# Variance along rows on one core: another split of columns between DVE, ACT and GpSimd, and the first loads' section under SP

## The chip, the cores and the metric

One core of a Trainium2 chip runs the program. The metric is the device time of one execution in microseconds. The kernel before takes 163.88 us, the median of 3 runs (163.84 to 163.9).

In the profile's names, ACT is ScalarE, DVE is VectorE, POOL is GpSimd, and SP is SyncE, which here issues the DMAs; "DVEq", "ACTq" and "SPq" are the instruction sequencers of the engines. TensorE is not used.

## The reference

```python
def setup_inputs():
    batch, seq, dim = 32, 512, 1024
    return {"x": np.random.randn(batch, seq, dim).astype(np.float32)}

def reference(x):
    mean_sq = np.mean(x**2, axis=-1)
    sq_mean = np.mean(x, axis=-1)**2
    return (mean_sq - sq_mean).astype(np.float32)
```

For each of 32 x 512 = 16384 rows of 1024 numbers the result is the mean of the squares less the square of the mean, that is, the variance of the row. The input is 67.1 MB, the output 65.5 KB.

## The kernel before

**Columns.** The 16384 rows are spread over 128 partitions and 128 columns: one column is one row of x on every partition, 128 x 1024 numbers in float32, 512 KB. All results stand in `mv[:, 1, c]`, one number per partition and column.

**Stages.** Columns 0 to 95 go through a loop in groups of 16 (`GROUP`), 8 MB a group, through two buffers `xt[0]` and `xt[1]` (`NBUF`). Three turns of the loop (`TURNS`) take two groups each. The 32 columns behind them (`END0` = 96 onwards) are the tail. It is loaded in eight loads of 8, 8, 5, 4, 2, 2, 1 and 1 columns (`END_LOADS`), and the very last column in two pieces of 512 numbers (`PIECES`). The first 16 tail columns go into `xt[0]`, the rest into `xt_end`.

**Two ways to a variance.** DVE takes a column with two `bn_stats` of 512 numbers each (the helper `halves`, line 118), and one `bn_aggr` that joins the two sets of statistics (line 225 in the loop, 253 and 267 in the tail). ACT takes a column with two passes: `act_mean` (line 122) sums the row into a scaled negative mean, `act_var` (line 127) squares the row with this mean as bias and sums again. Each pass is two instructions in the profile, an ACTIVATE and an ACTIVATION_READ_ACCUMULATOR that writes the sum. ACT works in batches: all means of a batch, a wait, all variances of it.

**Who takes what.** In the loop ACT has the first 6 of the 16 columns of a group (`NACT`), in two batches of 3 (`ACT_BATCH`), and DVE the other 10. In the tail, the string `END_WHO` gives each column of each load to A (ACT) or D (DVE). The first 11 D columns (`JOINED`, all those of the first two loads) get only their `bn_stats` on DVE; GpSimd joins their statistics in eleven small steps on all of them at once (lines 181 to 210), the last two of them writing one run of neighbouring columns each. For the other nine D columns DVE does the `bn_aggr` itself; it is put off behind the first `bn_stats` of the next column (`waiting`).

**Order.** All loads and stores are issued by SP, in program order, into one queue. The first two group loads stand in a `tile_critical` section (line 149), behind which the barriers of `tc.close()` and `tc.compile()` follow. Then SP loads a group as soon as the group two before it is finished: it waits on `done` (line 157). The first tail load waits for the fifth group (line 159); the other tail loads are issued right behind it.

In the loop DVE waits for the landing of a group, increments `go`, on which ACT starts its columns of that group, and does 20 `bn_stats` and 10 `bn_aggr`. Ahead of the last `bn_aggr` it waits for ACT's `act_done` (line 224); the last `bn_aggr` increments `done`. After every second group GpSimd copies the variances from `stage` to `mv` (line 174).

```python
            for j in mine:
                if j == mine[-1]:
                    take(dve, act_done, 1)
                last = dve.bn_aggr(out=stage[:, j, :], in_=stats[:, j, :, :])
            last.then_inc(done, 1)
```

DVE and ACT run through the tail in their own program order, each waiting for `landed_end[b]` ahead of its first column of load `b`. SP issues three stores: columns 0 to 15 (line 306), columns 16 to 120 when GpSimd's joined columns, ACT's of the first four loads and DVE's up to the fifth load are there (lines 307 to 310), and columns 121 to 127 when ACT and DVE are through (lines 311 to 313).

`addr_align` (line 147) places the code of ACT and DVE from that point on at instruction 128 of a fetch block.

Of the kernel before, what the change touches and what calls it, by code (L numbers as in the profile page):

```python
# [11 lines left out]
def kernel(  # L12
# [15 lines left out]
    P = nc.NUM_PARTITIONS  # L28
    FP32 = mybir.dt.float32
    ACTF = mybir.ActivationFunctionType  # L30
    ALU = mybir.AluOpType
    ENG = mybir.EngineType

    xf = x.flatten_outer_dims()
    N, D = xf.shape
    assert N % P == 0
    ncols = N // P
# [6 lines left out]
    GROUP = 16  # L44
    NBUF = 2
    TURNS = 3
    PER_TURN = NBUF * GROUP
    END0 = TURNS * PER_TURN
    NACT = 6
    ACT_BATCH = 3  # L50
    END_LOADS = [8, 8, 5, 4, 2, 2, 1, 1]
    END_WHO = "AADDDDDD" "AAADDDDD" "AADDD" "AADD" "DD" "AD" "D" "A"
    FIRST = END_LOADS[0] + END_LOADS[1]
    JOINED = END_WHO[:FIRST].count("D")
    PIECES = [512, 512]
    EARLY = 4
    HEAD = 128
# [1 line left out]
    def sbuf(name, shape, dtype):  # L59
        return nc.alloc_sbuf_tensor(name, shape, dtype).ap()  # L60

    def psum(name, shape, dtype):
        return nc.alloc_psum_tensor(name, shape, dtype).ap()

    xt = [sbuf(f"xt{b}", [P, GROUP, D], FP32) for b in range(NBUF)]
    xt_end = sbuf("xt_end", [P, ncols - END0 - FIRST, D], FP32)
    mv = sbuf("mv", [P, 2, ncols], FP32)
    stage = sbuf("stage", [P, PER_TURN, 2], FP32)
    stats = sbuf("stats", [P, PER_TURN, 2, 6], FP32)
    stats_join = sbuf("stats_join", [P, JOINED, 2, 6], FP32)  # L70
    stats_end = sbuf("stats_end", [P, ncols - END0, 4, 6], FP32)
    neg_mean = sbuf("neg_mean", [P, PER_TURN], FP32)
    neg_mean_end = sbuf("neg_mean_end", [P, ncols - END0], FP32)
    two = sbuf("two", [P, JOINED, 2], FP32)
    mu = sbuf("mu", [P, JOINED, 1], FP32)
    dev = sbuf("dev", [P, JOINED, 4], FP32)
    junk = [sbuf(f"junk{i}", [P, D], mybir.dt.bfloat16) for i in range(ACT_BATCH)]
    junk_sq = [psum(f"junk_sq{i}", [P, D], FP32) for i in range(ACT_BATCH)]

    sync, act, dve, gps = nc.sync, nc.scalar, nc.vector, nc.gpsimd  # L80
    landed = [nc.alloc_semaphore(f"landed{b}") for b in range(NBUF)]
    NEND = len(END_LOADS) + len(PIECES)
    landed_end = [nc.alloc_semaphore(f"landed_end{b}") for b in range(NEND)]
# [10 lines left out]
    def load(dst, c0, n, sem, f0=0, f=D):  # L94
        b0, pitch, row0 = next(b for b in BLOCKS if b[0] <= c0 < b[0] + b[1])
        assert c0 + n <= b0 + pitch
        ap = [[pitch * D, P], [D, n], [1, f]] if n > 1 else [[pitch * D, P], [1, f]]
        sync.dma_start(  # L98
            out=dst,
            in_=dataclasses.replace(xf, offset=(row0 + c0 - b0) * D + f0, ap=ap),  # L100
        ).then_inc(sem, 16)
# [10 lines left out]
    def take(engine, sem, n):  # L112
        engine.wait_ge(sem, n)
        engine.sem_inc(sem, -n)  # L114
# [6 lines left out]
    def act_mean(i, xcol, nm):  # L121
        return act.activation(  # L122
            out=junk[i], in_=xcol, func=ACTF.Copy, scale=-S / D, accum_out=nm
        )

    def act_var(i, xcol, nm, var):
        return act.activation(  # L127
            out=junk_sq[i], in_=xcol, func=ACTF.Square, scale=S, bias=nm, accum_out=var
        )

    def end_col(c):
        k = c - END0
        return xt[0][:, k, :] if k < FIRST else xt_end[:, k - FIRST, :]

    end_cols = []
    at = END0
    for b, n in enumerate(END_LOADS):
        end_cols += [(b, c, END_WHO[c - END0]) for c in range(at, at + n)]
        at += n
    assert at == ncols - 1 and sum(PIECES) == D  # L140
    early = END0 + sum(END_LOADS[:EARLY])
    act_step_of, dve_step_of = {}, {}
    joined = [c for b, c, who in end_cols if who == "D"][:JOINED]
    assert joined[-1] < END0 + FIRST and TURNS * NBUF >= NBUF + 1

    for engine in (act, dve):
        engine.addr_align(FETCH_BLOCK_INSTRUCTIONS, offset=HEAD, max_nops=0)

    with tc.tile_critical(sync_engine=ENG.Pool, no_gpsimd_drain=True):
        for g in range(NBUF):  # L150
            load(xt[g], g * GROUP, GROUP, landed[g])
    ctx.close()
# [7 lines left out]
    c = END0  # L160
    for b, n in enumerate(END_LOADS):
        k = c - END0
# [3 lines left out]
    f = 0  # L166
    for b, n in enumerate(PIECES, len(END_LOADS)):
        load(end_col(c)[:, f : f + n], c, 1, landed_end[b], f, n)
        f += n

    gps.sem_inc(copied, 1)
    for t in range(TURNS):
# [11 lines left out]
        lambda: gps.tensor_scalar(out=mu, in0=mu, scalar1=0.25, scalar2=None, op0=ALU.mult),  # L184
        lambda: gps.tensor_tensor(out=dev, in0=mean, in1=mu.to_broadcast([P, JOINED, 4]), op=ALU.subtract),
        lambda: gps.tensor_tensor(out=dev, in0=dev, in1=dev, op=ALU.mult),
# [25 lines left out]
    with nc.Fori(0, TURNS, engines=[ENG.DVE]):  # L212
        take(dve, copied, 1)
        for b in range(NBUF):
            take(dve, landed[b], 16)
            dve.sem_inc(go, 1)
            mine = range(b * GROUP + NACT, (b + 1) * GROUP)
            for j in mine:
# [11 lines left out]
    for b, c, who in end_cols:  # L230
        if who != "D":
            continue
        if b != seen:
            dve.wait_ge(landed_end[b], 16)
            seen = b
        col = end_col(c)
        if c in joined:
            last = halves(stats_join[:, joined.index(c), :, :], col)
            if c == joined[-1]:
                last.then_inc(dve_step, 1)  # L240
                n += 1
            continue
        st = stats_end[:, c - END0, :2, :]
        dve.bn_stats(out=st[:, 0, :], in_=col[:, :H])  # L244
        if waiting:
            waiting()
        n += 1
        dve.bn_stats(out=st[:, 1, :], in_=col[:, H:]).then_inc(dve_step, 1)  # L248
        dve_step_of.setdefault(b, n)

        def waiting(n=n, c=c, st=st):
            dve.wait_ge(dve_step, n)
            return dve.bn_aggr(out=mv[:, :, c], in_=st)  # L253

    c = ncols - 1
    st = stats_end[:, c - END0, : len(PIECES), :]
    f = 0
    for i, size in enumerate(PIECES):
        dve.wait_ge(landed_end[len(END_LOADS) + i], 16)
        last = dve.bn_stats(out=st[:, i, :], in_=end_col(c)[:, f : f + size])  # L260
        if i == 0:
            waiting()
        f += size
# [7 lines left out]
    with nc.Fori(0, TURNS, engines=[ENG.Activation]):  # L271
        for b in range(NBUF):
            take(act, go, 1)
            for i0 in range(0, NACT, ACT_BATCH):
                mine = range(b * GROUP + i0, b * GROUP + i0 + ACT_BATCH)
                for i, j in enumerate(mine):
                    last = act_mean(i, xt[b][:, i0 + i, :], neg_mean[:, j : j + 1])
                last.then_inc(act_step, 1)
                take(act, act_step, 1)
                for i, j in enumerate(mine):  # L280
                    last = act_var(
                        i, xt[b][:, i0 + i, :], neg_mean[:, j : j + 1], stage[:, j, 1:2]
                    )
            last.then_inc(act_done, 1)
    n = 0
    for b in range(len(END_LOADS)):
        mine = [c for bb, c, who in end_cols if bb == b and who == "A"]
# [59 lines left out]
```

## Time and profile before

| | before |
|---|---|
| median of 3 runs | 163.88 us (163.84 to 163.9) |
| the profiled execution | 163.92 us |
| its span | 162.6 us |
| instructions in the span | 570 |
| DVE busy | 103.8 us (64%), 232 instructions |
| ACT busy | 106.3 us (65%) |
| GpSimd busy | 3.6 us, 18 instructions |
| moved by DMA | 67.20 MB, 413 GB/s over the span |
| a `bn_stats` in the loop | 677 ns, x120 |
| an `act_mean`, an `act_var` | 1043 ns, 1104 ns |

The span runs from the first to the last instruction of the core; the execution's time has 1.3 us around it. A row of a timeline gives start and duration in us, the engine, the line of the kernel, the operation, what it writes and reads, and in brackets the idle time of the engine before it with what ended it. Neighbouring rows of one engine can overlap in time, since the next instruction begins before the one ahead of it has ended. A row of waits gives the waiting engine and line, the one it waited for, the time in total, the number of times and the longest. "DVEq L114" is DVE's own sequencer in `take`, which waits on a semaphore.

### The profile page before, as it was taken

To read this page: it belongs to the slowest core of one execution; us is meant where nothing else is said; L and a number is where in the kernel's file an instruction comes from. 1 tells how busy PE (TensorE), PEld (TensorE's weight loads), DVE (VectorE), ACT (ScalarE), POOL (GpSimd) and SP (SyncE) were. 2 spreads that over 40 slices of the span, in tenths; PEclk is the share of its full clock that TensorE was granted. 3 is DMA by queue.
4 is the path that set the end of the run, shared out by engine and by line. 5 is a ranking of instruction groups with operands and counts; after the bars stand their busy time and mean duration, and the time that the engine had idled before them with its cause. 6 is when DMAs were issued, how large, how long until landed. Compare 5 with 4: busy or idle time off the path is not lost. (4 is left out here: it accounts for less than half of the span.)

```text
span 162.6 us, 570 instructions
## 1 busy us (share of the span) xinstructions
DVE 103.8 (64%) x232; ACT 106.3 (65%) x189; POOL 3.6 (2%) x18
## 2 busy tenths in 40 slices
DVE  0000029980599607994099922998049979999994
ACT  3000029990599807995099932999149999799965
POOL 0000000000000000000000000000000000006000
DMA  7969979989998996996996997997989999999990
GB/s 262 516 290 484 516 322 451 516 355 419 516 419 355 516 484 290 516 500 274 516 500 274 516 516 306 468 516 339 435 387 427 468 395 417 448 416 409 414 356 7
DMA packets 2739, 67.20 MB, mean 413 GB/s; under 512 B 688, under 2 KB 688, under 8 KB 1200
## 3 DMA queue, kind: packets, MB, share of 16 engines
q1 hardware_dynamic: 2736, 67.18, 96.4%
q14 instruction: 3, 0.02, 0.1%
HBM read 67.11 MB, written 0.07 MB: 413 GB/s over the span
## 5 line engine op out<-in xcount | busy, mean ns | idle before, releaser
L118 DVE BATCH_NORM_STATS2 stats<-xt 128x6 f32<-128x512 f32 x120 | 71.8, 677 | 50.0 <-DVEq L114 50.0
L122 ACT ACTIVATE junk<-xt 128x1024 bf16<-128x1024 f32 x41 | 42.7, 1043 | 49.1 <-ACTq L114 48.0
L127 ACT ACTIVATE junk_sq<-xt,neg_mean 128x1024 f32<-128x1024 f32 x36 | 39.7, 1104 | 1.5
L118 DVE BATCH_NORM_STATS2 stats_join<-xt 128x6 f32<-128x512 f32 x22 | 13.2, 676 | 0.0
L225 DVE BATCH_NORM_AGGREGATE stage<-stats 128x2 f32<-128x12 f32 x60 | 6.0, 166 | 6.2 <-DVEq L114 5.3
L122 ACT ACTIVATION_READ_ACCUMULATOR junk<-xt 128x1 f32 x41 | 7.6, 186 | 0.0
L122 ACT ACTIVATE junk<-xt_end 128x1024 bf16<-128x1024 f32 x6 | 6.3, 1046 | 1.4 <-DMA xt_end<-in_x_dram 1.4
L127 ACT ACTIVATE junk_sq<-xt_end,neg_mean_end 128x1024 f32<-128x1024 f32 x6 | 6.7, 1110 | 0.1
L127 ACT ACTIVATION_READ_ACCUMULATOR junk_sq<-xt,neg_mean 128x1 f32 x36 | 6.7, 186 | 0.0
L244 DVE BATCH_NORM_STATS2 stats_end<-xt_end 128x6 f32<-128x512 f32 x9 | 6.1, 678 | 0.4 <-DMA xt_end<-in_x_dram 0.4
L248 DVE BATCH_NORM_STATS2 stats_end<-xt_end 128x6 f32<-128x512 f32 x9 | 5.8, 642 | 0.0
L127 ACT ACTIVATE junk_sq<-xt,neg_mean_end 128x1024 f32<-128x1024 f32 x5 | 5.5, 1105 | 0.1
L174 POOL COPY mv<-stage 128x32 f32<-128x32 f32 x3 | 0.6, 209 | 133.2 <-DVE stage L225 133.2
L270 ACT ACT_TABLE_LOAD x1 | 1.3, 1283 | 2.8 <-PEq L154 2.8
L253 DVE BATCH_NORM_AGGREGATE mv<-stats_end 128x2 f32<-128x12 f32 x9 | 1.7, 192 | 0.0
L260 DVE BATCH_NORM_STATS2 stats_end<-xt_end 128x6 f32<-128x512 f32 x2 | 1.3, 669 | 0.5 <-DMA xt_end<-in_x_dram 0.5
L127 ACT ACTIVATION_READ_ACCUMULATOR junk_sq<-xt_end,neg_mean_end 128x1 f32 x6 | 1.1, 187 | 0.0
L122 ACT ACTIVATION_READ_ACCUMULATOR junk<-xt_end 128x1 f32 x6 | 1.1, 186 | 0.0
L127 ACT ACTIVATION_READ_ACCUMULATOR junk_sq<-xt,neg_mean_end 128x1 f32 x5 | 0.9, 187 | 0.0
L182 POOL TENSOR_TENSOR two<-stats_join 128x22 f32<-128x22 f32 x1 | 0.3, 252 | 12.9 <-DVE stats_join L118 12.9
L201 POOL TENSOR_SCALAR mv<-mu 128x6 f32<-128x6 f32 (+1 forms) x2 | 0.5, 237 | 0.2
L187 POOL TENSOR_SCALAR dev<-dev 128x44 f32<-128x44 f32 x1 | 0.3, 332 | 0.1
(12 smaller groups left out, 2.3 us busy)
## 6 DMA issues: line engine op xcount, KB each, us to landing
xt<-in_x_dram SPq DMA_DIRECT2D x2, 4096.0 KB, 19.5
xt_end<-in_x_dram SPq DMA_DIRECT2D x1, 2560.0 KB, 29.8
xt_end<-in_x_dram SPq DMA_DIRECT2D x1, 2048.0 KB, 34.1
xt_end<-in_x_dram SPq DMA_DIRECT2D x2, 1024.0 KB, 37.2
xt_end<-in_x_dram SPq DMA_DIRECT2D x2, 512.0 KB, 40.4
xt_end<-in_x_dram SPq DMA_DIRECT2D x2, 256.0 KB, 40.9
xt<-in_x_dram SPq DMA_DIRECT2D x6, 24.5
out_dram<-mv SPq DMA_DIRECT2D x1, 52.5 KB, 5.3
```

The source lines that it names most:

```text
L118: last = dve.bn_stats(out=st[:, h, :], in_=xcol[:, h * H : (h + 1) * H])
L122: return act.activation(out=junk[i], in_=xcol, func=ACTF.Copy, scale=-S / D, accum_out=nm)
L127: return act.activation(out=junk_sq[i], in_=xcol, func=ACTF.Square, scale=S, bias=nm, accum_out=var)
L174: gps.tensor_copy(out=mv[:, 1, t * PER_TURN : (t + 1) * PER_TURN], in_=stage[:, :, 1]).then_inc(copied, 1)
L182: lambda: gps.tensor_tensor(out=two, in0=mean[:, :, 0:2], in1=mean[:, :, 2:4], op=ALU.add),
L201: lambda j=j, c=c, n=n: gps.tensor_scalar(out=mv[:, 1, c : c + n], in0=mu[:, j : j + n, 0], scalar1=1.0 / D, scalar2=None, op0=ALU.mult,)
L225: last = dve.bn_aggr(out=stage[:, j, :], in_=stats[:, j, :, :])
L244: dve.bn_stats(out=st[:, 0, :], in_=col[:, :H])
L248: dve.bn_stats(out=st[:, 1, :], in_=col[:, H:]).then_inc(dve_step, 1)
L253: return dve.bn_aggr(out=mv[:, :, c], in_=st)
L260: last = dve.bn_stats(out=st[:, i, :], in_=end_col(c)[:, f : f + size])
L270: act.preload_act_table(ACTF.Square)
```

## The change

Three things are edited.

The section of the first two loads is entered under SP instead of GpSimd (`sync_engine`).

In the loop ACT takes 7 of 16 columns instead of 6, in a batch of 4 and one of 3; DVE takes 9 instead of 10. There are four scratch buffers of each kind instead of three.

In the tail the loads have 8, 7, 6, 4, 2, 2, 1 and 1 columns. DVE has 7, 4, 4, 2, 2, 1 and 1 of the first seven loads (before: 6, 5, 3, 2, 2, 1 and 1), ACT 1, 3, 2, 2, 0, 1, 0 and 1 (before: 2, 3, 2, 2, 0, 1, 0 and 1). All D columns of the first three loads are joined on GpSimd, 15 instead of 11. The last column moves from `xt_end` to the sixteenth place of `xt[0]`.

```diff
-    NACT = 6
-    ACT_BATCH = 3
-    END_LOADS = [8, 8, 5, 4, 2, 2, 1, 1]
-    END_WHO = "AADDDDDD" "AAADDDDD" "AADDD" "AADD" "DD" "AD" "D" "A"
+    NACT = 7
+    ACT_BATCHES = [(0, 4), (4, 7)]
+    END_LOADS = [8, 7, 6, 4, 2, 2, 1, 1]
+    END_WHO = "ADDDDDDD" "AAADDDD" "AADDDD" "AADD" "DD" "AD" "D" "A"
     FIRST = END_LOADS[0] + END_LOADS[1]
-    JOINED = END_WHO[:FIRST].count("D")
+    JOINED = END_WHO[: FIRST + END_LOADS[2]].count("D")
...
-    xt_end = sbuf("xt_end", [P, ncols - END0 - FIRST, D], FP32)
+    xt_end = sbuf("xt_end", [P, ncols - 1 - END0 - FIRST, D], FP32)
...
-    junk = [sbuf(f"junk{i}", [P, D], mybir.dt.bfloat16) for i in range(ACT_BATCH)]
-    junk_sq = [psum(f"junk_sq{i}", [P, D], FP32) for i in range(ACT_BATCH)]
+    junk = [sbuf(f"junk{i}", [P, D], mybir.dt.bfloat16) for i in range(4)]
+    junk_sq = [psum(f"junk_sq{i}", [P, D], FP32) for i in range(4)]
...
     def end_col(c):
         k = c - END0
+        if c == ncols - 1:
+            return xt[0][:, FIRST, :]
         return xt[0][:, k, :] if k < FIRST else xt_end[:, k - FIRST, :]
...
-    with tc.tile_critical(sync_engine=ENG.Pool, no_gpsimd_drain=True):
+    with tc.tile_critical(sync_engine=ENG.SP, no_gpsimd_drain=True):
...
-            for i0 in range(0, NACT, ACT_BATCH):
-                mine = range(b * GROUP + i0, b * GROUP + i0 + ACT_BATCH)
+            for i0, i1 in ACT_BATCHES:
+                mine = range(b * GROUP + i0, b * GROUP + i1)
```

More of the change, by code (lines that the diff above doesn't have):

```diff
@@ L143 @@
     joined = [c for b, c, who in end_cols if who == "D"][:JOINED]
-    assert joined[-1] < END0 + FIRST and TURNS * NBUF >= NBUF + 1
     for engine in (act, dve):
         engine.addr_align(FETCH_BLOCK_INSTRUCTIONS, offset=HEAD, max_nops=0)
-    with tc.tile_critical(sync_engine=ENG.Pool, no_gpsimd_drain=True):
+    with tc.tile_critical(sync_engine=ENG.SP, no_gpsimd_drain=True):
         for g in range(NBUF):
```

## The prediction

> **What bounds the kernel now.** First the page, for what is busy and what ended last.
>
> ```profile
> span 162.6 us, 570 instructions
> ...
> DMA  7969979989998996996996997997989999999990
> ...
> q1 hardware_dynamic: 2736, 67.18, 96.4%
> q14 instruction: 3, 0.02, 0.1%
> ...
> DMA xt_end<-in_x_dram 25%; SPq L98 2%; ACT junk_sq L127 1%; ACT junk L122 1%; DVE stage L225 0%
> ```
>
> The load queue is busy for 96.4% of the span and the chain that ended last runs over the tail's loads; only the last columns' arithmetic follows them. Then two load periods, one per buffer, as stretches (length, then busy time of each engine, the clock, the DMA share):
>
> ```profile
> 42.50:61.90 19.40, 12.97 (x31) 13.35 (x24) 0.21 (x1) 1.00 1.00 432
> 61.90:81.20 19.30, 12.95 (x30) 13.36 (x24) 0.00 (x0) 1.00 1.00 435
> ```
>
> DMA is at 1.00 throughout, DVE and ACT are idle for some 6 of 19.36 us. By this alone moving a column to ACT costs nothing. The list of waits says who waits for whom inside the loop:
>
> ```profile
> DVE stage L225 <- DVEq L114: 5.3, 6, 0.9
> ACT junk L122 <- DMA xt_end<-in_x_dram: 1.4, 2, 1.1
> DVE stats_end L260 <- DMA xt_end<-in_x_dram: 0.5, 1, 0.5
> DVE stats_end L244 <- DMA xt_end<-in_x_dram: 0.4, 1, 0.4
> ```
>
> Line 225's six waits of 0.9 us are `take(dve, act_done, 1)`: in every group DVE is done before ACT, and waits for ACT ahead of its last aggregate. And in the whole tail DVE waits for loads for 0.9 us only. The rows of ACT's last group and of DVE's tail, in order of time (start, duration):
>
> ```profile
> 121.05 1.04 ACT L122 ACTIVATE junk<-xt 128x1024 bf16<-128x1024 f32 x1
> ...
> 122.09 1.04 ACT L122 ACTIVATE junk<-xt 128x1024 bf16<-128x1024 f32 x1
> ...
> 124.49 1.10 ACT L127 ACTIVATE junk_sq<-xt,neg_mean 128x1024 f32<-128x1024 f32 x1
> ...
> 125.62 1.10 ACT L127 ACTIVATE junk_sq<-xt,neg_mean 128x1024 f32<-128x1024 f32 x1
> ...
> 133.41 0.18 ACT L127 ACTIVATION_READ_ACCUMULATOR junk_sq<-xt,neg_mean 128x1 f32 x1
> ...
> 133.74 0.21 DVE L225 BATCH_NORM_AGGREGATE stage<-stats 128x2 f32<-128x12 f32 x1 [0.88 <-DVEq L114]
> 133.92 13.15 DVE L118 BATCH_NORM_STATS2 stats_join<-xt 128x6 f32<-128x512 f32 x22
> ...
> 146.99 0.68 DVE L244 BATCH_NORM_STATS2 stats_end<-xt_end 128x6 f32<-128x512 f32 x1
> ...
> 157.44 0.69 DVE L244 BATCH_NORM_STATS2 stats_end<-xt_end 128x6 f32<-128x512 f32 x1 [0.38 <-DMA xt_end<-in_x_dram]
> ...
> 159.31 0.69 DVE L260 BATCH_NORM_STATS2 stats_end<-xt_end 128x6 f32<-128x512 f32 x1 [0.51 <-DMA xt_end<-in_x_dram]
> ...
> 160.71 0.21 DVE L267 BATCH_NORM_AGGREGATE mv<-stats_end 128x2 f32<-128x12 f32 x1
> 160.96 0.19 ACT L127 ACTIVATION_READ_ACCUMULATOR junk_sq<-xt_end,neg_mean_end 128x1 f32 x1
> 161.17 0.33 SPq L105 DMA_DIRECT2D out_dram<-mv  x1
> ```
>
> See three things. ACT's accumulator ends at 133.59, the waiting aggregate starts 0.15 later, DVE's tail 0.18 after that: ACT sets when DVE's tail begins. From 133.92 to 160.92 DVE is nearly solid. And the last store goes out at 161.17, with ACT's last result (161.15); DVE is only 0.23 us ahead of it.
>
> **Part 1: the seventh ACT column in the loop (lines 49, 50, 274 to 279).** DVE loses two stats and one aggregate a group, 2 x 0.594 (19 steps from 20 rows of 11.97 us, less the last one's 0.68) + 0.09 = 1.28 us. None of it is on the path: DVE waits for ACT there already, and now waits longer. ACT gains one mean (121.05 to 122.09: 1.04 us) and one variance (124.49 to 125.62: 1.13 us), 2.17 us a group; the number of batches, and so of waits between means and variances, stays two. So every `act_done`, every `done` and every load behind a `done` comes 2.17 later. In five groups this is hidden: `done` of the third group was at 75.9 and the next landing let DVE go on at 81.25, 5.4 us of room, 3.2 left. GpSimd's copy of `stage`, 0.21 us after every second `done`, moves with it inside the same room. After the sixth group nothing hides it: DVE's tail starts at 133.92 + 2.17 = 136.09, though the first end load landed at 129.44.
>
> **Part 2: the later load issues.** A load is issued at `done`, at 56.56 for example, while the load ahead of it finishes on the 16 DMA engines between 60.90 and 61.66 (its landing records). The lead shrinks from 4.3 to 5.1 us to 2.2 to 2.9 us. The nearest row for what a load needs is the first one: issued at 0.87, its first packets start at 1.89 and the last engine's at 2.93, so 1.0 to 2.1 us. I take no gap, since 2.2 is above 2.1. If a gap does open, it opens for every second load (the next has the gap as extra lead): up to three times, some 0.3 each by the spread of those packets, +0.9 us; the lower end is zero. The ten end loads also move 2.17 later; the last issue stood 7.4 us on a full queue, so it has that much room.
>
> **Part 3: the tail's division (lines 51 to 55).** DVE's columns go from 20 to 21, the joined ones from 11 to 15. A joined column costs two stats, 1.19 us ((146.99 - 133.92) / 11); one aggregated on DVE takes 1.257 (rows from 148.18 to 155.73, six steps). So 15 x 1.188 = 17.83, and the first own column starts at 136.09 + 17.83 = 153.92 (before 146.99). Six such columns follow, 1.19 for the first (no aggregate in it yet) and 1.257 for five: the two pieces of the last column start at 161.40. Before, their start and stop were 159.31 and 160.92, 1.61 us, so DVE ends at 163.01. No landing is late for this: the single columns landed at 157.42 and 158.70, the pieces at 159.28 and 159.95; the 7-column second load lands 1.2 us earlier than the 8-column one, the third holds the same total of 21. As a check: 2.17 + (8 stats x 0.594 - 3 x 1.257 = 0.98) - the 1.06 us that DVE's pitch lost to the two waits = 2.09, and 160.92 + 2.09 = 163.01.
>
> ACT's tail loses a column in the first load, 2.17, and starts 2.17 later: it stays with the loads and ends no later than 161.15. GpSimd's steps go from 11 to 12 (three runs of joined columns) on 60 elements a row instead of 44: 3.6 us before, about 4.3 now, from 154.0 to 158.4. Behind them on SP stands the 52.5 KB store, issued at 154.98 before and at 158.4 now; it landed at 160.31, just behind the loads, and now lands by about 161, under DVE's end. If GpSimd's steps lost their cover, they would have to be 4.7 us longer first.
>
> **Part 4: the program's length and the last landings.** From its branch at line 147 to its end DVE has 129 distinct instructions in the trace (77 to the end of the loop, 52 behind); six fewer in the loop and one fewer in the tail make 122. The trace has one 8192-byte packet on q14, the instruction queue, at 155.9, and from then on one of the 16 landing records of each load trails: the load of line 98 for the last D column has fifteen by 156.15 and the sixteenth at 157.42, 1.27 late, against 0.26 for the load before. If the packet goes, the last piece lands at about 158.8 instead of 159.95. The Trainium skill's page "Runtime: NRT & Kernel Launch", section "Instruction fetch mechanics", speaks against any such gain: crossing a block costs one bump of the queue and is mostly hidden. The row here shows 1.2 us on the loads' end, the page would make it nothing, and the forecast is the same by either. On the path both ends of this term, 0 and -1.2, are worth 0, because DVE reaches the pieces only at 161.40. ACT's four or so extra instructions could bring a packet of their own; the cover is 1.4 us (161.40 - 159.95), the price beyond it nothing in the likeliest case.
>
> **Part 5: the section under SP.** Before, SP's branch into it waits for GpSimd's increment. In the trace SP's branch starts at 0.72 us of the span, and so does ACT's, which waits for nothing of GpSimd's: there is little to win. The bounds are -0.12 (the time between branch and first load issue) and +0.08 (one more instruction of SP's, by the step between its neighbours); I take 0. The two loads in the section are unchanged, GpSimd's queue loses the entry and exit increments, and the exit is covered: DVE and ACT are through it at 2.8 and wait for data until 23.2.
>
> **Sum.** DVE ends at 163.01, SP sees it some 0.1 later (its wait, then the store), so the last store goes out at 163.10 instead of 161.17: +1.93 us. The profiled execution took 163.92 around its span of 162.6, 0.04 over the median of 163.88; 163.88 + 1.93 = 165.8 us, +1.2%.
>
> **The rivals.**
> *Not slower.* The entry to DVE's tail doesn't move, ACT's seventh column being absorbed somewhere. Then DVE ends at 163.01 - 2.17 = 160.84; with the last landings earlier, too, ACT ends near 160.0, and the store goes at 160.93: 163.6, within 0.2%. It decides below 0.24 us of slip; from 0.24 + 0.33 on the result is measurably slower. For it speaks only ACT's 5.7 us of idle time a group; against it, that this idle time lies before the landing, and the column can't start before it.
> *The queue runs dry.* Part 2's gaps come on top: 165.8 + 0.9 = 166.7. For it: a lead of 2.2 us against 2.1; against it: the first load's late engines are those with instruction packets at 1.75 and 1.91 beside them.
> *The change doesn't shorten what it says.* The packet at 155.9 stays or moves: by part 4 still 165.8, and told from the main case only by the landing records.
> *GpSimd or the middle store becomes the end.* It would need 4.7 us more than the rows give: 165.8 up.
>
> **How the numbers follow.** DVE's tail as the end, with or without the packet: 0.88. Queue dry as well: 0.06. Not slower: 0.04. Something that makes it faster by over 0.2% (0.33 us, about what can be told from no change here): 0.02. The likeliest case's own range is 165.5 to 166.2, from part 5's bounds, 0.1 on the store and 0.2 on ACT's batches of four and three. Half of the dry queue's +0.9 is taken in above, and 0.2 below for terms that no row shows: 165.3 to 166.4 once rounded outwards. Faster 0.02, same 0.04, slower 0.94.
>
> **What would show it.** Right: the wait at line 225 grows from 0.9 to some 4.4 us (2.17 + 1.28 + 0.9); the joined stats start near 136.1 and number 30; no DVE row of the tail waits for a load; the store follows DVE's line 267 near 163.1; the chain that ended last runs over DVE. Wrong: joined stats starting near 134, the tail's stats waiting for loads again, or load periods above 19.36 us (the dry queue).

## The result and the profile after

The changed kernel takes 168.09 us (median of 6 runs, 167.81 to 169.8), the kernel before 163.78 us in the same comparison. The ratio is 1.028, with an interval of 1.0238 to 1.0322: slower by 2.8%. The forecast was 165.8 us, with a range of 165.3 to 166.4. The direction was right, and so was what ends last; the loss forecast (1.9 us) was less than half of what came (4.3 us).

The page of the changed kernel, the lines that answer to those shown of before:

```profile
span 166.3 us, 570 instructions
...
q1 hardware_dynamic: 2736, 67.18, 95.2%
q14 instruction: 2, 0.02, 0.0%
...
DVE stats_join L118 11%; DVE stats_end L245 2%; DVE stats_end L249 2%; DVE stats_end L261 1%; DVE mv L254 0%; DVE mv L268 0%; DVE stage L226 0%; DVEq L213 0%
```

The chain that ended last has changed from the loads to DVE's tail, as forecast: `stats_join` (line 118) is now its largest part. The instruction queue has two packets instead of three; the one at 155.9 is gone. The list of waits shows DVE's wait inside the loop:

```profile
DVE stage L226 <- DVEq L114: 25.9, 6, 4.3
```

DVE waits 4.3 us a group for `act_done`, where it waited 0.9, and the list has no row of DVE's tail that waits for a load any more. But the load periods are not as before. The prediction shows the first two of four periods before; the other two were (columns as there, the last one is GB/s):

```profile
81.20:100.60 19.40, 12.96 (x30) 13.35 (x24) 0.21 (x1) 1.00 1.00 432
100.60:119.90 19.30, 12.96 (x30) 13.35 (x24) 0.00 (x0) 1.00 0.96 414
```

The same four periods of the changed kernel, cut at its landings:

```profile
42.50:61.90 19.40, 11.70 (x27) 15.52 (x28) 0.21 (x1) 1.00 1.00 432
61.90:81.20 19.30, 11.70 (x27) 15.52 (x28) 0.00 (x0) 1.00 1.01 431
81.20:102.00 20.80, 11.70 (x27) 15.52 (x28) 0.21 (x1) 1.00 0.96 406
102.00:121.60 19.60, 11.70 (x27) 15.52 (x28) 0.00 (x0) 1.00 0.97 413
```

The first two periods are those of before. The third takes 20.8 us at 406 GB/s, the fourth 19.6: some 1.7 us more together. DVE's last group began like this before:

```profile
119.96 11.96 DVE L118 BATCH_NORM_STATS2 stats<-xt 128x6 f32<-128x512 f32 x20 [5.36 <-DVEq L114]
```

The rows around DVE's last group and its end in the changed kernel, in order of time (22 of the 30 joined statistics stand in the first `stats_join` row, eight on `xt_end` follow it):

```profile
118.08 0.21 DVE L226 BATCH_NORM_AGGREGATE stage<-stats 128x2 f32<-128x12 f32 x1 [4.31 <-DVEq L114]
...
121.80 10.78 DVE L118 BATCH_NORM_STATS2 stats<-xt 128x6 f32<-128x512 f32 x18 [3.51 <-DVEq L114]
...
137.75 0.21 DVE L226 BATCH_NORM_AGGREGATE stage<-stats 128x2 f32<-128x12 f32 x1 [4.31 <-DVEq L114]
137.94 13.15 DVE L118 BATCH_NORM_STATS2 stats_join<-xt 128x6 f32<-128x512 f32 x22
...
155.75 0.68 DVE L245 BATCH_NORM_STATS2 stats_end<-xt_end 128x6 f32<-128x512 f32 x1
...
163.23 0.68 DVE L261 BATCH_NORM_STATS2 stats_end<-xt 128x6 f32<-128x512 f32 x1
...
164.60 0.21 DVE L268 BATCH_NORM_AGGREGATE mv<-stats_end 128x2 f32<-128x12 f32 x1
```

From these rows the loss of the profiled execution (168.07 - 163.92 = 4.15 us) can be put together:

| part | before | after | difference |
|---|---|---|---|
| DVE starts the last group | 119.96 | 121.80 | +1.84 |
| from there to DVE's tail | 13.96 | 16.14 | +2.18 |
| from there to DVE's end | 27.00 | 26.87 | -0.13 |
| from DVE's end to the last store (164.89) | 0.25 | 0.08 | -0.17 |
| outside the span | 1.31 | 1.74 | +0.43 |
| sum | | | 4.15 |

The second, third and fourth line are the forecast's +1.93 (measured 1.88). The first and the last are what it missed.

### The profile page after: what moved, and what is told of

It is laid out like the page before. It is cut to its first block, busy times and chain, and to the rows that moved or that the text cites. A ratio compares the mean times of both kernels' runs of the same rounds, so it can differ in the third digit from the quotient of the medians.

```text
span 166.3 us, 570 instructions
## 1 busy us (share of the span) xinstructions
DVE 97.0 (58%) x213; ACT 117.3 (71%) x209; POOL 4.0 (2%) x19
## 3 DMA queue, kind: packets, MB, share of 16 engines
q1 hardware_dynamic: 2736, 67.18, 95.2%
## 5 line engine op out<-in xcount | busy, mean ns | idle before, releaser
L118 DVE BATCH_NORM_STATS2 stats<-xt 128x6 f32<-128x512 f32 x108 | 64.7, 679 | 41.0 <-DVEq L114 41.0
L122 ACT ACTIVATE junk<-xt 128x1024 bf16<-128x1024 f32 x46 | 47.9, 1042 | 40.2 <-ACTq L114 38.9
L127 ACT ACTIVATE junk_sq<-xt,neg_mean 128x1024 f32<-128x1024 f32 x42 | 46.3, 1102 | 1.5
L122 ACT ACTIVATION_READ_ACCUMULATOR junk<-xt 128x1 f32 x46 | 8.6, 186 | 0.0
L127 ACT ACTIVATION_READ_ACCUMULATOR junk_sq<-xt,neg_mean 128x1 f32 x42 | 7.8, 186 | 0.0
L118 DVE BATCH_NORM_STATS2 stats_join<-xt_end 128x6 f32<-128x512 f32 x8 | 4.8, 676 | 0.0
L127 ACT ACTIVATE junk_sq<-xt,neg_mean_end 128x1024 f32<-128x1024 f32 x4 | 4.4, 1107 | 0.1
L245 DVE BATCH_NORM_STATS2 stats_end<-xt_end 128x6 f32<-128x512 f32 x6 | 4.0, 675 | 0.0
L249 DVE BATCH_NORM_STATS2 stats_end<-xt_end 128x6 f32<-128x512 f32 x6 | 3.9, 643 | 0.0
L261 DVE BATCH_NORM_STATS2 stats_end<-xt 128x6 f32<-128x512 f32 x2 | 1.3, 656 | 0.0
L202 POOL TENSOR_SCALAR mv<-mu 128x4 f32<-128x4 f32 (+1 forms) x3 | 0.7, 232 | 0.3
## 6 DMA issues: line engine op xcount, KB each, us to landing
xt<-in_x_dram SPq DMA_DIRECT2D x1, 4096.0 KB, 14.3
```

The lines of the kernel that those rows point to most:

```text
L118: last = dve.bn_stats(out=st[:, h, :], in_=xcol[:, h * H : (h + 1) * H])
L122: return act.activation(out=junk[i], in_=xcol, func=ACTF.Copy, scale=-S / D, accum_out=nm)
L127: return act.activation(out=junk_sq[i], in_=xcol, func=ACTF.Square, scale=S, bias=nm, accum_out=var)
L202: lambda j=j, c=c, n=n: gps.tensor_scalar(out=mv[:, 1, c : c + n], in0=mu[:, j : j + n, 0], scalar1=1.0 / D, scalar2=None, op0=ALU.mult,)
```

## The experiments

Besides the times, two numbers are used that are worked out from the DMA packet records of the traces. *Idle* is the time between 30 and 117 us, summed over the 16 DMA engines, in which fewer than 16 packets of the load queue were under way (one engine without a packet for 2 us counts as 2 us). *Slow* is the time by which 64 KB packets in the same stretch took longer than their usual 2.42 us, summed over those that were over 0.1 us late. Each load has 16 landing records; how far apart the first and the last of them are says how unevenly the engines work. The *lead* is the time from a load's issue to the first landing record of the load ahead of it; where a range is given, it is that of the loop's reissued loads. All ratios are to the kernel before, run on the same chip beside it.

### The three parts of the change, each by itself

The theory after the result: two losses, DVE's late entry to its tail (2.2 us) and a load queue that runs dry because `done`, and with it each load's issue, comes 2.17 us later (1.8 us). The rivals: the landings are late because of the section under SP, or because of the new tail's loads.

**The section alone.**

```diff
-    with tc.tile_critical(sync_engine=ENG.Pool, no_gpsimd_drain=True):
+    with tc.tile_critical(sync_engine=ENG.SP, no_gpsimd_drain=True):
```

> The kernel before with the first loads' section under SP and nothing else. Theory (loop and tail make the whole loss): 163.8 to 164.0 us, the first load issued 0.06 us later than before as in the changed kernel, landing records of each load 0.8 us apart as before. Rival (the section changes how the queue runs, and the spread of the landings comes from it): landings of the loop's loads up to 2 us apart, 165 us or more.

163.78 us, ratio 1.0004 (0.9994 to 1.0014). The first load goes out at 0.93 instead of 0.87, since SP now runs the section's increment itself (its row starts at 0.70); landing records are 0.9 us apart, idle and slow are 0. The section costs nothing that can be measured.

**The loop alone.**

```diff
-    NACT = 6
-    ACT_BATCH = 3
+    NACT = 7
+    ACT_BATCHES = [(0, 4), (4, 7)]
...
-            for i0 in range(0, NACT, ACT_BATCH):
-                mine = range(b * GROUP + i0, b * GROUP + i0 + ACT_BATCH)
+            for i0, i1 in ACT_BATCHES:
+                mine = range(b * GROUP + i0, b * GROUP + i1)
```

> The kernel before with ACT on 7 of 16 columns in the loop and the tail unchanged. Theory A (two losses: DVE's tail starts 2.17 us later, and the queue runs dry because the loads are issued 2.17 us later): by the tail alone DVE would end 2.17 - 1.06 = 1.1 us later, 164.8 us; with a gap in the queue like that of the changed kernel, 1.85 us, 166.6 us; a gap shows as landing records of one of the loop's loads more than 1.2 us apart and a last group later than 120.5. Theory B (the queue never runs dry, the late landings come from something in the tail or the section): 164.8 us and last group at 119.9.

166.65 us, ratio 1.0177 (1.0152 to 1.0203). This is theory A's number. Landing records of the fifth load are 1.85 us apart, idle is 6.4 us and slow 17.4 us, and the last group starts late:

```profile
121.77 10.78 DVE L118 BATCH_NORM_STATS2 stats<-xt 128x6 f32<-128x512 f32 x18 [3.44 <-DVEq L114]
```

121.77 against 119.96 before: the loop edit alone brings the whole delay of the loads.

**The tail alone.**

```diff
-    NACT = 7
-    ACT_BATCHES = [(0, 4), (4, 7)]
+    NACT = 6
+    ACT_BATCHES = [(0, 3), (3, 6)]
...
-    with tc.tile_critical(sync_engine=ENG.SP, no_gpsimd_drain=True):
+    with tc.tile_critical(sync_engine=ENG.Pool, no_gpsimd_drain=True):
```

(The diff is against the changed kernel.)

> The changed kernel with the loop's 6 ACT columns and the section under GpSimd put back, so the new tail alone. Theory: DVE's tail starts at 133.9 and needs 0.98 us more than before, the loop's loads land as before; DVE ends near 160.9, and whether the 8192-byte packet on the instruction queue goes or stays, the time is 163.4 to 163.9 us. Rival (the new tail costs the 1.85 us, through its loads): 165 us or more, last group landed as before but end loads late.

163.43 us, ratio 0.9988 (0.9978 to 0.9998), at the low end of what was expected. No gaps, DVE's tail starts at 133.72 and DVE ends at 160.60. The packet on the instruction queue comes at 161.8, behind all loads, and the landing records of the last loads are 0.6 us apart instead of 1.7; the last piece lands at 158.83, not 159.95. The new tail costs nothing, it gains some 0.1%; it is the loop edit that costs.

### The queue against the entry

Now the two losses were taken away one at a time from the changed kernel, with ACT's seven columns left as they are.

**A longer lead, the entry as it is.** DVE's nine columns of a buffer are free some 5 us before ACT's seven. So each load is cut in two, and DVE's part is issued when DVE's statistics are done. The tail's first load goes to DVE's places. (Against the changed kernel; the same cut of the first two loads and the tail's places are left out here.)

```diff
+    freed = nc.alloc_semaphore("freed")
...
-        sync.wait_ge(done, g - NBUF + 1)
-        load(xt[g % NBUF], g * GROUP, GROUP, landed[g % NBUF])
-    sync.wait_ge(done, (TURNS - 1) * NBUF + 1)
+        b = g % NBUF
+        sync.wait_ge(freed, g - NBUF + 1)
+        load(xt[b][:, NACT:, :], g * GROUP + NACT, GROUP - NACT, landed[b])
+        sync.wait_ge(done, g - NBUF + 1)
+        load(xt[b][:, :NACT, :], g * GROUP, NACT, landed[b])
+    sync.wait_ge(freed, (TURNS - 1) * NBUF + 1)
...
-            take(dve, landed[b], 16)
+            take(dve, landed[b], 32)
...
             take(dve, dve_step, 1)
+            dve.sem_inc(freed, 1)
```

> The changed kernel with each group's load cut in two: DVE's nine columns are reloaded when DVE's statistics are done, some 5 us before ACT's seven, which are reloaded when the group is done as before; the tail's first load goes into DVE's places and needs DVE alone. The lead of the loads grows from 2.1 us to 7 us. Theory (the queue ran dry): landing records 0.8 us apart in all loads, last group at 119.9 to 120.1, and the time is the forecast's 165.8 to 166.0 us: 2.1 us less than the changed kernel. Rival (the loads are slowed by ACT's and DVE's work or by the new load sizes, not by a dry queue): 167.5 us or more, landings up to 2 us apart.

166.39 us (166.32 to 166.45), ratio 1.0167 (1.0147 to 1.0187). The loads now go out 7.7 us or more ahead. Idle is 0 and no packet is slow (they have 36 and 28 KB here, usually take 1.37 and 1.06 us, and none took 0.02 us more); landing records are 0.5 to 0.6 us apart in all loads of the loop and the tail. The same four periods of this kernel:

```profile
42.70:62.10 19.40, 11.70 (x27) 15.52 (x28) 0.21 (x1) 1.00 1.00 432
62.10:81.50 19.40, 11.70 (x27) 15.52 (x28) 0.00 (x0) 1.00 1.00 432
81.50:101.00 19.50, 11.70 (x27) 15.52 (x28) 0.21 (x1) 1.00 1.00 430
101.00:120.40 19.40, 11.70 (x27) 15.52 (x28) 0.00 (x0) 1.00 1.00 429
```

DVE and ACT do the very same work in each period (11.70 and 15.52 us), yet the third period is back at 19.5: it isn't ACT's or DVE's work that slows the loads. That it is the lead and not the size of the loads is shown further below, by kernels that only delay the issue. The time is 0.4 us over the expected 165.8 to 166.0. Against the kernel before, the last group lands 0.51 us later (120.24, not 119.73, with 3600 packets on the queue instead of 2736), the delay growing from 0.15 at the first group by 0.07 with each further one; and the time outside the span is 0.15 us longer. The runs now agree within 0.13 us, where those of the changed kernel are 2 us apart.

**An earlier entry, the loads not cut.** DVE no longer waits for ACT; SP and GpSimd wait for `act_done` themselves.

```diff
         sync.wait_ge(done, g - NBUF + 1)
+        sync.wait_ge(act_done, g - NBUF + 1)
...
         gps.wait_ge(done, (t + 1) * NBUF)
+        gps.wait_ge(act_done, (t + 1) * NBUF)
...
-                if j == mine[-1]:
-                    take(dve, act_done, 1)
```

> The changed kernel, but DVE doesn't wait for ACT's act_done ahead of a group's last aggregate; SP (for the reload) and GpSimd (for its copy) wait for act_done themselves. The lead of the loads stays at 2.1 us. Theory (two separate losses, DVE's late entry to the tail and the dry queue): the entry moves up by 4.3 us, so the tail is bound by the loads again, and these still come some 1.2 to 1.9 us late: last column's pieces at 160.5 to 162.1, 165.0 to 166.0 us. Rival (the queue is not what is left; the entry alone makes the loss): 163.5 us or less. Second rival (DVE's waiting isn't on the path): 168 us as the changed kernel.

165.33 us (164.74 to 166.53), ratio 1.0107 (1.0064 to 1.0151), inside the expectation of the two losses. DVE's tail starts at 134.02 although the last group comes only at 122.41. The lead is 2.4 to 3.0 us, somewhat longer than the 2.0 to 2.4 of the changed kernel. Idle is 1.3 us, slow 16.6 us, the last piece lands at 161.43. Now ACT ends last, behind a late load:

```profile
122.41 10.77 DVE L118 BATCH_NORM_STATS2 stats<-xt 128x6 f32<-128x512 f32 x18 [9.49 <-DVEq L114]
...
134.02 8.35 DVE L118 BATCH_NORM_STATS2 stats_join<-xt 128x6 f32<-128x512 f32 x14
...
161.30 1.12 ACT L127 ACTIVATE junk_sq<-xt_end,neg_mean_end 128x1024 f32<-128x1024 f32 x1
...
162.36 0.19 ACT L127 ACTIVATION_READ_ACCUMULATOR junk_sq<-xt_end,neg_mean_end 128x1 f32 x1
162.57 0.33 SPq L105 DMA_DIRECT2D out_dram<-mv  x1
```

**Both.** The edits of the last two together.

> The changed kernel with both: DVE without the wait for act_done, and the loads cut in two with the long lead. Theory: neither loss is left; the loads end as with the split alone (last pieces at 159.5, last A column at 158.2), ACT ends 2.4 us behind its column at 160.6, 163.0 to 163.3 us. Rival (ACT's seventh column costs something beside these two): above 164 us.

163.73 us, ratio 1.0008 (0.9999 to 1.0017): neither loss is left. It is 0.4 us above the expected 163.0 to 163.3, and its time outside the span is 1.74 us, as in the changed kernel, against 1.31 before. The four kernels make a square:

| | short lead | long lead |
|---|---|---|
| DVE waits for `act_done` | 1.028 (the changed kernel) | 1.0167 |
| DVE doesn't wait | 1.0107 | 1.0008 |

The short lead costs 1.0 to 1.1% (1.6 to 1.8 us) in either row, the wait 1.6 to 1.7% in either column: within the intervals (up to 0.4% to either side) the two losses add up. The square is not quite clean: the lead differs between the two kernels on the left, and the right column bears the 0.5 us of the cut loads, so the lead's own price may be larger by that.

### How much lead a load needs

The kernel before, with scratch work on ACT in each group that only delays `act_done`.

**A whole mean pass more, 1.04 us.**

```diff
...
+                if i0:
+                    last = act_mean(3, xt[b][:, 0, :], neg_mean[:, PER_TURN : PER_TURN + 1])
                 last.then_inc(act_step, 1)
```

> The kernel before with one more mean pass of ACT per group, into scratch (work added that the result doesn't need): act_done, and so every reload, comes 1.04 us later, the lead is 3.2 us instead of 4.3. DVE's tail starts 1.04 us later, which its 1.06 us of waits for loads take up. If a lead of 3.2 us is enough: landings 0.8 us apart in the loop, 163.5 to 163.8 us. If the queue runs dry at 3.2 us already: landings of the fifth or sixth group over 1.2 us apart and 164 us or more.

164.42 us (163.57 to 164.46), ratio 1.0029 (1.0011 to 1.0048). The queue does run dry, a little: idle 1.5 us, slow 3.9 us, gaps at 60.6 of up to 0.77 us. The time is that of the second case, the spread of the loop's landings (at most 0.93) stays under what was written for it. In the waits, DVE's for `act_done` has grown by the pass:

```profile
DVE stage L225 <- DVEq L114: 11.7, 6, 2.0
```

**Half a pass more.** The same on 512 numbers; the issues come 0.33 us later than before.

> The kernel before with half a mean pass more of ACT per group (512 numbers, into scratch; work added that the result doesn't need), about 0.6 us: the loads are issued some 3.4 to 3.8 us ahead of the first engine that runs out, where one whole pass left 3.0 and 16 landings of up to 1.0 us apart after gaps of up to 0.8 us. Theory (an issue needs up to 3.7 us to reach the last engine while the queue runs): gaps of 0.3 us at most or none, 163.6 to 163.9 us. Rival (any shorter lead than before costs): gaps as with a whole pass, 164.2 us or more.

163.81 us, ratio 0.9999 (0.999 to 1.0009), idle 0, slow 0. Put in order of the lead:

| | lead, us | idle, us | slow, us |
|---|---|---|---|
| before | 4.3 | 0 | 0 |
| half a pass more | 4.0 | 0 | 0 |
| a whole pass more | 3.2 to 3.5 | 1.5 | 3.9 |
| DVE without the wait | 2.4 to 3.0 | 1.3 | 16.6 |
| the loop alone | 2.3 to 2.4 | 6.4 | 17.4 |
| changed kernel, section under GpSimd | 2.1 to 2.3 | 4.2 | 14.3 |
| changed kernel | 2.0 to 2.4 | 4.0 | 10.8 |

Between 4.0 and 3.3 us the queue begins to suffer. Below that the lead alone doesn't say by how much. In the changed kernel the tail's first load, behind the stretch counted here, has a lead of 1.4 us only, and between 117 and 125 us another 7.3 us of idle follow; there it costs nothing, since DVE's tail waits for no load.

### A kernel that beats both, and the time outside the span

**The new tail, six ACT columns, DVE without the wait.** The section under SP, and then the same with it under GpSimd. (Against the changed kernel.)

```diff
-    NACT = 7
-    ACT_BATCHES = [(0, 4), (4, 7)]
+    NACT = 6
+    ACT_BATCHES = [(0, 3), (3, 6)]
...
         sync.wait_ge(done, g - NBUF + 1)
+        sync.wait_ge(act_done, g - NBUF + 1)
...
-                if j == mine[-1]:
-                    take(dve, act_done, 1)
```

> The new tail and the section under SP, ACT with 6 columns as before, and DVE without the wait for act_done: a lead of 4.3 us and an earlier entry to the tail. Theory: the entry is 0.9 us earlier than before, DVE's program of fewer than 128 instructions has no instruction packet in the tail, the last A column lands at 157.5 and the last piece at 158.8; ACT ends at 159.9 and DVE at about the same, 162.3 to 162.6 us, 1.0 us under the kernel before. Rival (the loads' end doesn't move, because the packet stays or because it isn't what makes the sixteenth landing late): 163.3 us or more.

163.07 us, ratio 0.9963 (0.9949 to 0.9976): faster than the kernel before by 0.4%, between the 1.0 us expected and the rival's 163.3 or more. Inside the span the 1.0 us is all there:

```profile
132.67 2.42 DVE L118 BATCH_NORM_STATS2 stats_join<-xt 128x6 f32<-128x512 f32 x4
...
157.56 1.06 ACT L122 ACTIVATE junk<-xt_end 128x1024 bf16<-128x1024 f32 x1
...
159.64 0.21 DVE L269 BATCH_NORM_AGGREGATE mv<-stats_end 128x2 f32<-128x12 f32 x1
159.80 0.19 ACT L127 ACTIVATION_READ_ACCUMULATOR junk_sq<-xt_end,neg_mean_end 128x1 f32 x1
160.01 0.33 SPq L105 DMA_DIRECT2D out_dram<-mv  x1
```

DVE enters its tail at 132.67, the last A column's pass starts at 157.56, both engines end together, and the last store goes 1.16 us earlier than before (161.17). But the time outside the span is 1.59 us instead of 1.31.

> ACT with 6 columns, the new tail, DVE without the wait for act_done, and the section under GpSimd as before. With the section under SP this took 163.07 us: a span of 161.45 and 1.59 us outside it, against 1.31 outside in the kernel before. Theory A (the 0.3 us outside come from the section under SP together with the short program): 1.31 outside, first load 0.06 us earlier, 162.7 us. Theory B (they come from the new tail alone): 1.6 outside, 163.0 us.

163.17 us, ratio 0.9964 (0.995 to 0.9978), with a profiled execution of 163.3 around a span of 161.6: 1.7 outside. The section isn't the reason: by theory A it would have been 1.31.

> The changed kernel with the section put back under GpSimd. The queue still runs dry and DVE's tail still starts late: 167.4 to 168.3 us. Theory A (section under SP and short program together make the time outside the span longer, 1.74 against 1.31): 1.3 outside and 167.6 us or so. Theory B (not the section): 1.7 outside and 168.0 us.

167.98 us, ratio 1.0273 (1.0249 to 1.0297), 167.58 around 165.85: 1.73 outside. So the section is no part of it here either, and the rest of the changed kernel's loss stays. Theory B as it was written, the new tail alone, doesn't hold: the kernel with the tail alone has 1.31. What adds 0.15 to 0.43 us outside the span of seven kernels here, the changed one among them, remains open.

## Why the prediction was right and where it was wrong

**Part 1, the seventh column: right.** The entry to DVE's tail moved by 2.18 us against its last group (2.17 forecast), the wait at the last aggregate grew to 4.3 us (4.4). The long lead with the wait left in costs 1.67%, only a part of which is the cut of the loads (0.5 us, 0.3%); so this loss stands by itself.

**Part 2, the later load issues: wrong, and the step that failed.** The working took the need of a load from the first one of the kernel, issued into idle engines, 1.0 to 2.1 us, found the lead of 2.2 just above it, and took no gap. The lead came out near that, 2.0 to 2.4 us (issues 2.31 us later than before, 39.52 against 37.21, since the first group itself started 0.15 later). It is the need that was wrong: a load that is issued behind a running one can need more. The packet records put in 16 chains, each packet next to the one that ended last before it (the records don't name the engine, so this is worked out, not read), show the late engines going on 3.1 us after the issue in the changed kernel (78.22 to 81.27), and 3.7 with the loop alone (77.88 to 81.54) and with one more pass (57.59 to 61.33). Why it takes them longer there isn't shown. The price was undersized with it: up to 0.9 us for gaps, where 1.84 was measured. The price had only gaps in it, and idle engines are the smaller part: 4.0 us over 16 engines, while packets around the gaps took up to 3.3 us instead of 2.42, 10.8 us together. And the slowest engine decides, not the mean, since a group lands with its last record: (4.0 + 10.8) / 16 is only 0.9 us, but the sixteenth record of the last group came at 121.58 instead of 119.73. The rival "the queue runs dry" was the right one, priced at half and given 6 in 100.

**Part 3, the division of the tail: right.** 17.81 us from the first joined column to the first own one (17.83), 7.48 to the first piece (7.48), 1.58 to the end (1.61). GpSimd's steps took 155.92 to 160.02, 4.1 us (4.3), and the middle store went at 160.04, well under DVE's end.

**Part 4, the program's length: right, and off the path as said.** The packet at 155.9 went with the shorter program. What it is worth is seen where the loads are the end: with it (the section alone) the last loads' landing records are 1.85 us apart, without it ahead of the loads' end (the tail alone) 0.6, and the last piece lands at 158.8 instead of 160.0. Its fifteenth record comes at 158.8 in both; only the sixteenth moves. With one more pass the packet comes at 157.18, with half a pass at 156.02, and the sixteenth record falls behind from the following load on. The Trainium skill's page "Runtime: NRT & Kernel Launch", section "Instruction fetch mechanics", calls the cost of a crossing mostly hidden; here it is hidden for DVE, whose rows have no idle time beside the packet, but it shows in one of the sixteen landing records of each load, by 1.2 us.

**Part 5, the section: right.** +0.06 us at the first issue, inside the bounds of -0.12 and +0.08, nothing in the time.

**The sum: a term was missing.** The time around the span was taken as unchanged; it grew by 0.43 us, and no run explains it. The range, too, doesn't follow from its parts: with half of the 0.9 us for the dry queue on top of the likeliest case's 166.2 it would have ended near 166.7, not 166.4; the result lies above either.

## What to carry to other kernels

When a change delays the signal that frees a buffer, measure the lead of the next load against a load issued behind a running one, not against the first load of the kernel; here 4.0 us were enough and 3.3 were not. An engine that closes a loop by waiting for another one carries the other's extra work into everything that it does afterwards: let those who need both wait for both, and the engine itself goes on. A column is not free on an engine with idle time if that idle time lies before its data.

## What the hardware showed that was not expected

- From a load's issue to the engines' first packets: 1.0 to 2.1 us for the first load, up to 3.7 us for the late engines behind a running load. Not every short lead does harm: in the changed kernel the loads issued at 39.52 and 58.87, with leads of 2.0 and 2.15 us, left no engine idle; the one issued at 78.22, with 2.15 us again, did. Why it is the later ones there, and already the second reissued load with one more pass, was not settled.
- Around such gaps packets are slow: up to 4.06 us for 64 KB, which otherwise take 2.42 (DVE without the wait, short lead).
- In the changed kernel what has fallen behind stays behind: the landing records are about 2 us apart from the fifth load to the last. It need not: with the loop alone they go from 1.85 us in the fifth load to 1.25 in the tail.
- The time outside the span differs between kernels, 1.31 to 1.74 us.
